# Weight sums by accumulating DMA, another order of Strassen's products, and another order of the last units of a feed-forward network

## Chip, core and metric

The kernel runs on one core of a Trainium2 chip. The metric is the device time of one execution in microseconds (us), the median of several runs. The core has five instruction queues that matter here. TensorE (PE in the profile, with PEld for its weight loads) does the matmuls. VectorE (DVE) and ScalarE (ACT) do elementwise work. GpSimd (POOL) does small work and can issue DMA transfers. SyncE (SP) issues most of the loads. Each queue is worked off in order. A DMA issued from any queue runs on the same 16 DMA engines.

## The reference

Two decoder layers over 256 tokens of width 1024, in float32. Cut to the part that the change touches:

```python
def swiglu(x, w1, w3, w2):
    return (jax.nn.silu(x @ w1) * (x @ w3)) @ w2

for i in range(DEPTH):                     # DEPTH = 2
    h = h + 0.5 * swiglu(rms_norm(h, g_ffn1[i]), w1_a[i], w3_a[i], w2_a[i])
    u = rms_norm(h, g_mix[i])
    h = h + hybrid_mixer(u, ...)           # three attention branches, gates, w_out
    h = h + 0.5 * swiglu(rms_norm(h, g_ffn2[i]), w1_b[i], w3_b[i], w2_b[i])
    h = h + sigmoid(rms_norm(h, g_ple[i]) @ w_ple_gate[i]) * (p[i] @ w_ple_proj[i])
out = rms_norm(h, g_final)
```

The hidden width of the feed-forward network (FFN) is 2816. There are four FFNs in a run: layer 0 a and b, layer 1 a and b.

## The kernel before

**Precision.** Every float32 operand is split into a high and a low float32r part: an ACT cast makes the high part (`whi`, `xhi`, `fhi`), and a DVE subtraction the low one (`wlo`, `xlo`, `flo`). One product is then three matmuls (`mm3`, lines 102 to 104). Weights come in tiles of 128 x 1024 (512 KB). `load` (lines 85 to 87) loads one into `raw` (4 buffers) and splits it; `split_w` splits a tile that is in SBUF already, through `split_T` (lines 135 and 136). Both write into the same 7 pairs of `whi` and `wlo`, so ACT and DVE can run at most 7 tiles ahead of TensorE.

**One FFN.** `ffn` cuts the hidden width into 11 chunks of 256 columns. For a chunk c, "up" makes the 256 gate columns and the 256 value columns side by side (512 columns) from all of D = 1024, for both blocks of 128 tokens. `gated` makes silu(gate) times value of one token block: an ACT activation, then a DVE operation into `pr` (lines 236 to 238). `turn(c)` transposes the two `pr` tiles of a chunk on TensorE (line 250, four transposes) and splits the result into `fhi` and `flo`. `down_unit(c, j)` loads one tile of w2 and adds its product with half a chunk to the four `acc` banks of PSUM (12 matmuls). Chunks 0 to 2 go up in the ordinary way at the start of the FFN; chunks 3 to 6 go up in quarters, `up_unit(c, i, os)` (one weight tile, 12 matmuls each).

**Strassen pairs.** Chunks 7 and 8, and 9 and 10, are made in pairs. The input is seen as a 2 x 2 matrix of blocks (token block by half of D), and the weights of two chunks as a 2 x 2 matrix of quarters (half of D by chunk, two 128 x 1024 tiles each). Seven products of quarters stand for eight. `x_forms` makes the sums of the input once per FFN. `winograd` loads the eight weight tiles of a pair (`wr`, line 317), `form` makes sums of quarters with DVE (line 320, in place or into `t2s`), `make(i)` splits the operand of product i, and the generator `products` runs the products: 12 matmuls each, into a PSUM bank of the tag `tr`, which the transposes use as well (2 banks). Line 345 adds a bank to an earlier result on DVE, and line 352 copies product 1 out on ACT.

**Order.** `block` writes the order out by hand. In step k it calls `make` for the product after next in its list, `form(k + 2)`, the next product, one quarter of an ordinary up, and a unit of down and turns as its two dictionaries say. One call to `block` covers one pair; an FFN has two calls. The second pair's loads are issued in step 6 of the first block. After the second block come the down units of chunks 5 and 6 with turns 6, 10 and 9 among them, and last the downs of chunks 9 and 10, which close the four `acc` banks one after the other. The framework puts waits where the data need them, hands out buffers as they come free, and may move independent instructions within a queue; the order above is its starting point.

**Beyond the FFN.** `mixer` does the attention branches and `ple` the embedding gate. `norm_r` (lines 164 to 175) computes the factor of the next RMSNorm from the finished rows, with small operations on POOL.

Of the kernel before, what the change touches and what calls it, by code (L numbers as in the profile page):

```python
# [33 lines left out]
def trunk(ctx: ExitStack, tc: tile.TileContext, a: dict, out: bass.AP):  # L34
# [10 lines left out]
    def nm(s):  # L45
        n_tile[0] += 1
        return f"{s}_{n_tile[0]}"
# [143 lines left out]
    def ffn(li, w13, w2, r, g, first=False, aside=None):  # L191
        nonlocal ident
        with tc.tile_pool(name=nm("fp"), bufs=3) as fp:

            def wtile():
                return fp.tile([P, U], F32, tag="wr", name=nm("wr"), bufs=10)

            def t512(name):
                return fp.tile([P, 512], F32, tag="t512", name=nm(name), bufs=4)
# [67 lines left out]
            def x_forms():  # L267
# [31 lines left out]
                V.tensor_tensor(out=s1, in0=a10, in1=a11, op=ALU.add)  # L299
# [5 lines left out]
                sub(a01, a01, s1)  # L305
# [5 lines left out]
            def winograd(c, fx):  # L311
                ws, t2s, fw = [], [], {}
                for u in range(2):
                    ws.append({(kh, nh): wtile() for kh in range(2) for nh in range(2)})
                for kh, nh in ((0, 0), (1, 0), (0, 1), (1, 1)):
                    for u in range(2):
                        nc.sync.dma_start(ws[u][kh, nh], w13[li, c + nh, 2 * kh + u])

                def sub(out, a, b):
                    V.tensor_tensor(out=out, in0=a, in1=b, op=ALU.subtract)  # L320


                def form(i):
                    for u, w in enumerate(ws):
                        if i == 1:
                            sub(w[0, 0], w[0, 1], w[0, 0])
                        elif i == 2:
                            t2s.append(wtile())
                            sub(t2s[u], w[1, 1], w[0, 0])
                        elif i == 3:  # L330
                            sub(w[0, 1], w[1, 1], w[0, 1])
                        else:
                            sub(w[1, 0], w[1, 0], t2s[u])
# [10 lines left out]
                def add(out, a, b):  # L344
                    V.tensor_tensor(out=out, in0=a, in1=b, op=ALU.add)


                def products():
                    o = bank_tr()
# [7 lines left out]
                    o = bank_tr()  # L357
# [7 lines left out]
                    o = bank_tr()  # L365
                    product(o, 5, True)
                    c22 = t512("c22")
                    add(c22, o, m1)
                    gated(c + 1, 1, c22, r[0])
                    yield  # L370
                    product(o, 3)
                    add(u2, o, u2)
                    gated(c + 1, 0, u2, r[0])
                    yield
                    o = bank_tr()
                    product(o, 4, True)
                    add(m1, o, m1)
# [3 lines left out]
                return make, form, products()  # L381


            def block(wg, plain, turns, downs, then=None):
                make, form, ps = wg
                following = None
                os = []
                for k in range(8):
                    if k < 6:
                        make((2, 6, 7, 5, 3, 4)[k])  # L390
                    if k < 3:
                        form(k + 2)
                    if k == 6 and then is not None:
                        following = winograd(then, fx)
                    if k == 7 and then is not None:
                        following[0](1)
                        following[1](1)
                    if k < 7:
                        next(ps)
                    if k % 4 == 0:  # L400
                        os = []
                    up_unit(plain[k // 4], k % 4, os)
                    if k in downs:
                        down_unit(*downs[k])
                    for t in turns.get(k, ()):
                        turn(t)
                return following

            for c in range(3):
# [21 lines left out]
            wg[1](1)  # L431
            for j in range(2):
                down_unit(0, j)
            if first:
                later()
            wg = block(
                wg, (3, 4), {0: [2], 4: [3]},
                {0: (1, 0), 1: (1, 1), 2: (2, 0), 3: (2, 1), 5: (3, 0), 6: (3, 1)}, 9,
            )
            if aside is not None:  # L440
                aside()
            block(
                wg, (5, 6), {0: [4], 1: [7], 2: [8], 5: [5]},
                {1: (4, 0), 2: (4, 1), 3: (7, 0), 4: (7, 1), 5: (8, 0), 6: (8, 1)},
            )
# [673 lines left out]
```

## Time and profile before

| | before |
|---|---|
| median of 3 runs | 1333.01 us (1332.68 to 1333.23) |
| the profiled execution, its time | 1332.86 us |
| its span, first to last instruction | 1331.1 us |
| TensorE matmul busy | 1312.2 us, 6624 matmuls |
| TensorE weight loads busy | 1097.5 us |
| VectorE busy | 994.0 us |
| ScalarE busy | 802.8 us |
| GpSimd busy | 50.2 us |
| read from HBM | 234.40 MB |
| granted TensorE clock | 0.998 |

Busy time is the time in which an engine executed an instruction; matmuls overlap each other, so a busy TensorE may still be issuing more slowly than it could. A row of a group reads: line, engine, operation, out<-in with the program's names, count, then busy time in us, mean ns of one, idle time of the engine just before them and what ended it. A row of the timeline reads: start in us, duration in us, engine, line, operation, count, and in brackets the idle time before it with the instruction that ended it.

### The profile page before, as it was taken

To read this page: it belongs to the slowest core of one execution; us is meant where nothing else is said; L and a number is where in the kernel's file an instruction comes from. 1 tells how busy PE (TensorE), PEld (TensorE's weight loads), DVE (VectorE), ACT (ScalarE), POOL (GpSimd) and SP (SyncE) were. 2 spreads that over 40 slices of the span, in tenths; PEclk is the share of its full clock that TensorE was granted. 3 is DMA by queue.
4 is the path that set the end of the run, shared out by engine and by line. 5 is a ranking of instruction groups with operands and counts; after the bars stand their busy time and mean duration, and the time that the engine had idled before them with its cause. 6 is when DMAs were issued, how large, how long until landed. Compare 5 with 4: busy or idle time off the path is not lost.

```text
span 1331.1 us, 17969 instructions
## 1 busy us (share of the span) xinstructions
PE 1312.2 (99%) x6624; PEld 1097.5 (82%) x6624; DVE 994.0 (75%) x1414; ACT 802.8 (60%) x1205; POOL 50.2 (4%) x109
## 2 busy tenths in 40 slices
PE   9999999999999999999999999999999999999997
PEld 7788879978888888887888888898888788888876
DVE  7998755666768789975789986566676677999755
ACT  6665546665775655654756665466667835655645
POOL 1000000001100000000100000000010000000001
PEclk9999999999999999999999999999999999999999
DMA  8774537534455567455566646373444465583542
GB/s 296 274 269 127 187 103 228 171 123 132 147 169 175 161 227 276 122 164 182 163 239 196 217 128 210 103 224 127 159 142 143 144 204 167 206 299 102 180 145 80
DMA packets 67769, 236.63 MB, mean 178 GB/s; under 512 B 8160, under 2 KB 8800, under 8 KB 67680
## 3 DMA queue, kind: packets, MB, share of 16 engines
q1 hardware_dynamic: 67104, 234.39, 54.0%
q8 instruction: 52, 0.85, 0.3%
q10 hardware_dynamic: 576, 1.08, 0.2%
q14 instruction: 37, 0.30, 0.1%
HBM read 234.40 MB, written 1.05 MB: 177 GB/s over the span
## 4 chain that ended last, share of the span: by engine, by line
PE 94%; ACT 2%; DVE 2%; DMA 1%; issue 1%; POOL 0%; SPq 0%; POOLq 0%; ACTq 0%; DVEq 0%
PE mm L102 17%; PE mm L104 17%; PE mm L103 17%; PE acc L102 8%; PE acc L103 8%; PE acc L104 8%; PE tr L104 4%; PE tr L102 4%; PE tr L103 4%; PE tr L250 1%; PE tr L150 1%; ACT whi L86 1%; PE tr L716 1%; DVE wlo L87 1%; DMA h<-in_x 1%
## 5 line engine op out<-in xcount | busy, mean ns | idle before, releaser
L87 DVE TENSOR_TENSOR wlo<-raw,whi 128x1024 fp32r<-128x1024 f32 (+1 forms) x378 | 450.1, 1201 | 137.3 <-ACT whi L86 135.1
L86 ACT CAST whi<-raw 128x1024 fp32r<-128x1024 f32 (+1 forms) x378 | 387.3, 1035 | 198.2 <-PE mm L104 77.5
L102 PE MATMUL mm<-whi,xhi 128*128 128x512 f32 (+1 forms) x760 | 296.0, 393 | 0.0
L103 PE MATMUL mm<-wlo,xhi 128*128 128x512 f32 (+1 forms) x760 | 295.1, 389 | 0.3 <-DVE wlo L87 0.3
L104 PE MATMUL mm<-whi,xlo 128*128 128x512 f32 (+1 forms) x760 | 295.2, 389 | 0.0
L102 PEld LDWEIGHTS mm<-whi,xhi 128*128 128x128 f32 x760 | 143.0, 188 | 30.0 <-DVE sqk L516 0.7
L104 PEld LDWEIGHTS mm<-whi,xlo 128*128 128x128 f32 x760 | 142.8, 188 | 29.7 <-DVE xlo L136 0.7
L103 PEld LDWEIGHTS mm<-wlo,xhi 128*128 128x128 f32 x760 | 142.9, 188 | 28.9 <-DVE wlo L87 0.8
L135 ACT CAST whi<-wr 128x1024 fp32r<-128x1024 f32 (+1 forms) x120 | 121.6, 1023 | 66.9 <-PE acc L104 38.9
L136 DVE TENSOR_TENSOR wlo<-wr,whi 128x1024 fp32r<-128x1024 f32 (+1 forms) x120 | 140.6, 1185 | 24.8 <-ACT whi L135 23.6
L102 PE MATMUL acc<-whi,fhi 128*128 128x512 f32 x352 | 132.0, 393 | 7.7 <-ACT fhi L135 7.7
L103 PE MATMUL acc<-wlo,fhi 128*128 128x512 f32 x352 | 137.9, 392 | 0.4 <-DVE wlo L87 0.4
L104 PE MATMUL acc<-whi,flo 128*128 128x512 f32 x352 | 134.6, 390 | 0.0
L102 PEld LDWEIGHTS acc<-whi,fhi 128*128 128x128 f32 x352 | 65.7, 188 | 23.2 <-ACT fhi L135 9.6
L103 PEld LDWEIGHTS acc<-wlo,fhi 128*128 128x128 f32 x352 | 66.1, 188 | 15.2 <-DVE wlo L87 1.8
L104 PEld LDWEIGHTS acc<-whi,flo 128*128 128x128 f32 x352 | 66.1, 188 | 13.6
L320 DVE TENSOR_TENSOR wr<-wr,wr 128x1024 f32<-128x1024 f32 x64 | 76.3, 1217 | 0.0
L102 PE MATMUL mm<-xhi,whi 128*128 128x256 f32 x256 | 73.8, 288 | 0.0
L104 PE MATMUL mm<-xhi,wlo 128*128 128x256 f32 x256 | 72.5, 283 | 0.0
L103 PE MATMUL mm<-xlo,whi 128*128 128x256 f32 x256 | 72.4, 283 | 0.0
L102 PE MATMUL tr<-whi,q 128*128 128x512 f32 x160 | 63.7, 398 | 0.0
L104 PE MATMUL tr<-whi,q 128*128 128x512 f32 x160 | 62.6, 391 | 0.0
(248 smaller groups left out, 1960.8 us busy)
## 6 DMA issues: line engine op xcount, KB each, us to landing
raw<-in_w13b SPq DMA_DIRECT2D x56, 512.0 KB, 3.7
raw<-in_w13a SPq DMA_DIRECT2D x52, 512.0 KB, 4.2
raw<-in_wg SPq DMA_DIRECT2D x48, 512.0 KB, 3.7
raw<-in_w2a SPq DMA_DIRECT2D x44, 512.0 KB, 4.4
raw<-in_w2b SPq DMA_DIRECT2D x44, 512.0 KB, 4.3
wr<-in_w13a SPq DMA_DIRECT2D x32, 512.0 KB, 6.7
raw<-in_wqk SPq DMA_DIRECT2D x32, 512.0 KB, 4.1
wr<-in_w13b SPq DMA_DIRECT2D x32, 512.0 KB, 6.2
```

What stands on the lines that cost most here:

```text
L86: A.copy(hi[:, c], raw[:, c])
L87: V.tensor_tensor(out=lo[:, c], in0=raw[:, c], in1=hi[:, c].bitcast(F32), op=ALU.subtract)
L102: PE.matmul(o, lhs[0], rhs[0], start=first, stop=False, **more)
L103: PE.matmul(o, lhs[0], rhs[1], start=False, stop=False, **more)
L104: PE.matmul(o, lhs[1], rhs[0], start=False, stop=last, **more)
L135: A.copy(hi, t)
L136: V.tensor_tensor(out=lo, in0=t, in1=hi.bitcast(F32), op=ALU.subtract)
L150: PE.transpose(t[:, j * P : (j + 1) * P], h[tb][:, k * P : (k + 1) * P], ident)
L250: PE.transpose(t[:, j * S + tb * P : j * S + (tb + 1) * P], prs[c, tb][:, j * P : (j + 1) * P], ident)
L320: V.tensor_tensor(out=out, in0=a, in1=b, op=ALU.subtract)
L716: PE.transpose(t[:, j * P : (j + 1) * P], e[:, j * P : (j + 1) * P], ident)
```

## The change

`winograd` becomes `pair`. It loads a pair's quarters into x (upper half of D, first chunk), y (lower, first), w (upper, second) and z (lower, second), and makes sums of quarters in place by DMA transfers on POOL's queue that add a tile from memory to the tile in SBUF: w + upper first (for product 5), then w + lower second (6), then w + lower first (4); z + upper second (7). `form`, `t2s` and the DVE subtractions of line 320 go. A sum is issued after the split of the tile's earlier content. Signs in `x_forms` change with it, and so does the order of the products: 1, 2, 5, 3, 6, 7, 4 instead of 1, 2, 6, 7, 5, 3, 4. Products 5 and 3 are copied out by ACT and later subtracted on DVE. The first pair's tiles are loaded in the order w, x, y, z. The second pair's loads are issued one quarter at a time, with the products 5, 3, 6 and 7 (steps 2 to 5). `wr` gets 12 buffers instead of 10, `t512` 5 instead of 4.

`block` now walks a list: S is the next Strassen product, P a quarter of an ordinary up, D a unit of down, T a turn. The units behind the blocks stand in another order as well.

```diff
             def wtile():
-                return fp.tile([P, U], F32, tag="wr", name=nm("wr"), bufs=10)
+                return fp.tile([P, U], F32, tag="wr", name=nm("wr"), bufs=12)
...
-                V.tensor_tensor(out=s1, in0=a10, in1=a11, op=ALU.add)
+                sub(s1, a10, a11)
...
-                sub(a01, a01, s1)
+                V.tensor_tensor(out=a01, in0=a01, in1=s1, op=ALU.add)
...
+            ORDER = (1, 2, 5, 3, 6, 7, 4)
+
+            def pair(c, bank):
+                def at(kh, nh, u):
+                    return w13[li, c + nh, 2 * kh + u]
+
+                t = {q: [wtile() for _ in range(2)] for q in "xywz"}
+                fw = {}
+                quarters = {"x": (0, 0), "y": (1, 0), "w": (0, 1), "z": (1, 1)}
+
+                def fetch(q):
                     for u in range(2):
-                        nc.sync.dma_start(ws[u][kh, nh], w13[li, c + nh, 2 * kh + u])
...
+                        nc.sync.dma_start(t[q][u], at(*quarters[q], u))
+
+                def plus(q, kh, nh):
+                    for u in range(2):
+                        nc.gpsimd.dma_start(t[q][u], at(kh, nh, u), accum_op=ALU.add)
 
                 def make(i):
-                    at = {1: (0, 0), 2: (1, 0), 7: (0, 1), 5: (0, 0), 3: (1, 1), 4: (1, 0)}
-                    fw[i] = [split_w(t2s[u] if i == 6 else w[at[i]]) for u, w in enumerate(ws)]
+                    q = {1: "x", 2: "y", 5: "w", 3: "z", 6: "w", 7: "z", 4: "w"}[i]
+                    fw[i] = [split_w(w) for w in t[q]]
+                    if i == 5:
+                        plus("w", 1, 1)
+                    elif i == 3:
+                        plus("z", 0, 1)
+                    elif i == 6:
+                        plus("w", 1, 0)
...
+                    product(o, 5, True)
+                    c5 = t512("c5")
+                    A.copy(c5, o)
+                    yield
+                    product(o, 3)
+                    v = t512("v")
+                    A.copy(v, o)
+                    yield
+                    o = bank()
                     product(o, 6, True)
                     u2 = t512("u2")
-                    add(u2, o, m1)
+                    sum_(u2, o, m1)
+                    sum_(v, v, u2, ALU.subtract)
+                    gated(c + 1, 0, v, r[0])
                     yield
                     product(o, 7)
-                    add(m1, o, m1)
+                    sum_(m1, o, m1)
+                    sum_(c5, c5, m1, ALU.subtract)
+                    gated(c + 1, 1, c5, r[0])
...
+                for kind, *arg in plan:
+                    if kind == "S":
+                        if k < 6:
+                            make(ORDER[k + 1])
+                        if then is not None:
+                            if k == 2:
+                                following = pair(*then)
+                                following[1]("w")
+                            elif k == 3:
+                                following[1]("x")
+                                following[2]()
...
-                    wg = winograd(7, fx)
+                    wg = pair(7, bank_tr)
+                    for q in "wxyz":
+                        wg[1](q)
+                    wg[2]()
...
+            wg = block(wg, [
+                ("S",), ("P", 3, 0), ("D", 1, 0), ("T", 2), ("S",), ("P", 3, 1), ("D", 1, 1), ("S",),
+                ("P", 3, 2), ("D", 2, 0), ("S",), ("P", 3, 3), ("D", 2, 1), ("S",), ("P", 4, 0), ("T", 3),
+                ("S",), ("P", 4, 1), ("D", 3, 0), ("S",), ("P", 4, 2), ("D", 3, 1), ("P", 4, 3),
+            ], (9, bank_tr))
...
+            wg = block(wg, [
+                ("S",), ("P", 5, 0), ("T", 4), ("S",), ("P", 5, 1), ("D", 4, 0), ("T", 7), ("S",), ("P", 5, 2),
+                ("D", 4, 1), ("T", 8), ("S",), ("P", 5, 3), ("D", 7, 0), ("S",), ("P", 6, 0), ("D", 7, 1),
+                ("S",), ("P", 6, 1), ("T", 5), ("D", 8, 0), ("S",), ("P", 6, 2), ("D", 8, 1), ("P", 6, 3),
+            ])
...
-            for j in range(2):
-                down_unit(5, j)
-            turn(6)
-            turn(10)
-            for j in range(2):
-                down_unit(6, j)
-            turn(9)
+            block((None, None, None, iter(())), [
+                ("D", 5, 0), ("T", 10), ("D", 5, 1), ("T", 6), ("T", 9), ("D", 6, 0), ("D", 6, 1),
+            ])
```

`first_sum`, the third function that `pair` returns, is `plus("w", 0, 0)`.

More of the change, by code (lines that the diff above doesn't have):

```diff
@@ L195, in wtile @@
             def wtile():
-                return fp.tile([P, U], F32, tag="wr", name=nm("wr"), bufs=10)
+                return fp.tile([P, U], F32, tag="wr", name=nm("wr"), bufs=12)
             def t512(name):
-                return fp.tile([P, 512], F32, tag="t512", name=nm(name), bufs=4)
+                return fp.tile([P, 512], F32, tag="t512", name=nm(name), bufs=5)
             if first:
@@ L342, in product, with sum_ @@
                         mm3(o, [y[:, kt, :] for y in fx[i]], m, start and kt == 0, kt == 3, skip_group_check=True)
-                def add(out, a, b):
-                    V.tensor_tensor(out=out, in0=a, in1=b, op=ALU.add)
+                def sum_(out, a, b, op=ALU.add):
+                    V.tensor_tensor(out=out, in0=a, in1=b, op=op)
                 def products():
-                    o = bank_tr()
+                    o = bank()
                     product(o, 1, True)
@@ L356, in products @@
                     yield
-                    o = bank_tr()
+                    o = bank()
+                    product(o, 5, True)
[6 more added lines that the diff above has]
+                    yield
+                    o = bank()
                     product(o, 6, True)
                     u2 = t512("u2")
-                    add(u2, o, m1)
+                    sum_(u2, o, m1)
@@ L361, in products @@
+                    sum_(v, v, u2, ALU.subtract)
+                    gated(c + 1, 0, v, r[0])
                     yield
                     product(o, 7)
-                    add(m1, o, m1)
+                    sum_(m1, o, m1)
+                    sum_(c5, c5, m1, ALU.subtract)
+                    gated(c + 1, 1, c5, r[0])
                     yield
[L365 to L375, printed above, removed]
+                    o = bank()
                     product(o, 4, True)
-                    add(m1, o, m1)
+                    sum_(m1, o, m1)
                     gated(c, 1, m1, r[0])
                     yield
-                return make, form, products()
@@ L384, in block, with first_sum @@
-            def block(wg, plain, turns, downs, then=None):
-                make, form, ps = wg
+                def first_sum():
+                    plus("w", 0, 0)
+                return make, fetch, first_sum, products()
+            def block(now, plan, then=None):
+                make, _, _, ps = now
                 following = None
                 os = []
[L388 to L398, printed above, removed]
-                        next(ps)
[L400 to L406, printed above, removed]
+                k = 0
+                for kind, *arg in plan:
[9 more added lines that the diff above has]
+                                following[2]()
+                            elif k == 4:
+                                following[1]("y")
+                            elif k == 5:
+                                following[1]("z")
+                            elif k == 6:
+                                following[0](1)
+                        next(ps)
+                        k += 1
+                    elif kind == "P":
+                        if arg[1] == 0:
+                            os = []
+                        up_unit(*arg, os)
+                    elif kind == "D":
+                        down_unit(*arg)
+                    else:
+                        turn(*arg)
@@ L430, in ffn @@
             wg[0](1)
-            wg[1](1)
             for j in range(2):
```

26 lines of the change are left out of this document (removed).

## The prediction

> **What bounds the kernel now.** I read the page first: busy times and the group of each matmul line. Then busy time by window over one feed-forward stage, the waits, and the timeline of the places where TensorE stood still.
>
> ```profile
> PE 1312.2 (99%) x6624; PEld 1097.5 (82%) x6624; DVE 994.0 (75%) x1414; ACT 802.8 (60%) x1205; POOL 50.2 (4%) x109
> ...
> L102 PE MATMUL acc<-whi,fhi 128*128 128x512 f32 x352 | 132.0, 393 | 7.7 <-ACT fhi L135 7.7
> ...
> L320 DVE TENSOR_TENSOR wr<-wr,wr 128x1024 f32<-128x1024 f32 x64 | 76.3, 1217 | 0.0
> ```
> ```profile
> 701.00:764.00 63.00, 63.00 (x283) 51.91 (x282) 60.10 (x61) 38.43 (x45) 0.00 (x0) 1.00 0.61 201
> 764.00:831.00 67.00, 66.34 (x305) 54.76 (x303) 50.39 (x55) 39.56 (x48) 0.00 (x0) 1.00 0.55 167
> ```
>
> The window rows give start:end, length, then busy time of PE, PEld, DVE, ACT and POOL with their counts, granted clock, DMA share and GB/s. They cover the two Strassen blocks of the third FFN. TensorE is the bound. In the first block it never rests: 63 us hold 283 matmuls, one every 63 / 283 = 0.223 us, so a unit of 12 matmuls takes 2.67 us. The clock is granted in full. DVE is close behind (60.10 of 63), but nobody waits for it there. The change keeps every matmul: seven products a pair, the same up and down units, the same transposes. So it can only win time in which TensorE stands, and 1331.1 - 1312.2 = 18.9 us of visible idle is a ceiling, most of it outside the edited code. Inside it, two kinds of stall matter.
>
> The first is at the end of each FFN:
>
> ```profile
> PE acc L102 <- ACT fhi L135: 7.7, 8, 1.2
> ```
> ```profile
> 121.17 0.60 PE L250 MATMUL tr<-ident,pr 128*128 128x128 f32 x4
> 121.52 0.48 PE L102 MATMUL tr<-whi,q 128*128 128x512 f32 x1
> ```
> ```profile
> 171.59 1.04 PE L250 MATMUL tr<-ident,pr 128*128 128x128 f32 x8
> 171.78 1.05 ACT L86 CAST whi<-raw 128x1024 fp32r<-128x1024 f32 x1 [1.67 <-PE acc L104]
> 172.74 1.07 ACT L135 CAST fhi<-tr 128x512 fp32r<-128x512 f32 x2
> 173.37 0.50 PE L102 MATMUL acc<-whi,fhi 128*128 128x512 f32 x1 [0.74 <-ACT fhi L135]
> ...
> 178.96 0.60 PE L250 MATMUL tr<-ident,pr 128*128 128x128 f32 x4
> 179.16 1.04 ACT L86 CAST whi<-raw 128x1024 fp32r<-128x1024 f32 x1 [1.67 <-PE acc L104]
> 180.11 0.58 ACT L135 CAST fhi<-tr 128x512 fp32r<-128x512 f32 x1
> 180.74 0.50 PE L102 MATMUL acc<-whi,fhi 128*128 128x512 f32 x1 [1.18 <-ACT fhi L135]
> ```
>
> The waits row reads: in total, times, longest. Eight stalls, two in each of four FFNs. A turn (four transposes) is followed at once by a down matmul that reads what the turn made, and the cast of it sits behind a 1.05 us weight cast that the last down released. Where other work follows a turn, the next matmul starts 0.35 us after the first transpose (121.17 to 121.52); at the last turn it starts 1.78 us after (178.96 to 180.74). The last turn loses 1.78 - 0.35 = 1.43 us start to start, 1.18 of it as visible idle.
>
> The second is the start of the first block of layer 0, three short stalls:
>
> ```profile
> 46.17 0.50 PE L102 MATMUL tr<-whi,xhi 128*128 128x512 f32 x1 [0.56 <-ACT m L352]
> 47.09 0.50 PE L103 MATMUL acc<-wlo,fhi 128*128 128x512 f32 x1 [0.41 <-DVE wlo L87]
> ...
> 55.63 0.50 PE L103 MATMUL mm<-wlo,xhi 128*128 128x512 f32 x1 [0.33 <-DVE wlo L87]
> ```
>
> **The change, part by part.**
>
> *The tail.* Before: both units of down 5, turn 6, turn 10, both of down 6, turn 9, then the last downs, which begin with chunk 9. After: a unit of 5, turn 10, a unit of 5, turn 6, turn 9, both units of 6, the last downs. Turn 9 now has two units, 5.3 us, ahead of its first reader; the 1.2 us from weight cast to end of its cast fits. Turn 6 is still followed by one other turn and then by its own down, as turn 6 and turn 10 were: the 0.74 us stall stays. Gain 4 x 1.43 = 5.7 us (4 x 1.18 = 4.7 by visible idle, the lower end). The loads and casts of the tail are the same ones; turn 10, now alone, costs what turn 9 alone cost.
>
> *Sums off DVE.* 64 tensor operations of 1217 ns go (the L320 row), 76.3 us of DVE. They lie beside TensorE, so they gain nothing by themselves, except the two stalls on DVE wlo above: 0.41 + 0.33 = 0.74 us, once.
>
> *Sums by DMA.* Each pair gets eight transfers of 512 KB on POOL's queue that add into a tile that a plain load, or an earlier sum, filled. Before, POOL issued no DMA, so their price has to be bounded.
>
> ```profile
> 10.00:20.00 10.00, 10.00 (x46) 8.29 (x45) 8.48 (x14) 6.83 (x15) 3.87 (x3) 1.00 1.03 411
> ```
> ```profile
> raw<-in_w13b SPq DMA_DIRECT2D x56, 512.0 KB, 3.7
> ...
> wr<-in_w13a SPq DMA_DIRECT2D x32, 512.0 KB, 6.7
> wr<-in_w13b SPq DMA_DIRECT2D x32, 512.0 KB, 6.2
> ```
> ```profile
> DMA to landing us min/median/max: 4.0/6.4/9.9
> ```
>
> With the DMA engines full, 411 GB/s: a 512 KB load holds them 0.524 MB / 411 GB/s = 1.28 us. Low end 1.28 us of engine time and 4.0 us to landing; high end 9.9 us, the longest landing of a load into these tiles. I take the wr row, 6.4 us to landing, as the nearest (same tile, same size, in a queue). A sum that is needed has this long:
>
> ```profile
> 121.36 1.05 ACT L135 CAST whi<-wr 128x1024 fp32r<-128x1024 f32 x1 [1.67 <-PE acc L104]
> ...
> 130.01 1.05 ACT L135 CAST whi<-wr 128x1024 fp32r<-128x1024 f32 x1 [1.67 <-PE acc L104]
> ...
> 138.65 1.05 ACT L135 CAST whi<-wr 128x1024 fp32r<-128x1024 f32 x1 [1.31 <-PE acc L104]
> ```
> ```profile
> 124.28 1.23 DVE L136 TENSOR_TENSOR wlo<-wr,whi 128x1024 fp32r<-128x1024 f32 x1
> ```
>
> Casts of successive products start 8.65 us apart (121.36, 130.01, 138.65). In the new order a tile is split, added into and split again two products later: w for 5, 6 and 4, z for 3 and 7. The last reader of the first split ends at 124.28 + 1.23 = 125.51, the second following cast starts at 138.65: 13.1 us for two transfers. At 6.4 us, even one after the other (12.8), they fit: price nothing. That cover gone, ACT stands in its queue ahead of the next turn's cast; the shortest way from a turn to its down (turn 3, turn 4) is two units, 5.3 us. So TensorE stops only when two transfers take over 13.1 + 5.3 = 18.4 us. At the high end, 2 x 9.9 = 19.8, it loses 1.4 us in each of 24 chains (three a pair): 34 us.
>
> Engine time: block one has the DMA busy 0.61 of 63 us, 24.6 us free; it issues eight sums, so each may hold the engines 3.1 us. The rule that speaks against the change is in the Trainium skill, "Collectives: The Full Stack", Part 3, on the fold count: an add in the DMA reads two sources through the same read ring, so it runs at half a copy's rate. By it a sum would hold the engines 2.56 us, eight of them 20.5 of the 24.6 free us, and the sum here would not move except at the starts below; by the row alone it is 10.2 us. No run before shows which.
>
> *Loads in another order, 12 tiles for 10.* The first pair's loads now go w, x, y, z, where x, the first product's quarter, went first; and the two sums into w compete with x, y, z.
>
> ```profile
> 474.30 8.60 SPq L317 DMA_DIRECT2D wr<-in_w13b  x8
> ```
> ```profile
> 483.65 1.99 ACT L135 CAST whi<-wr 128x1024 fp32r<-128x1024 f32 x2
> 485.54 2.00 ACT L86 CAST whi<-raw 128x1024 fp32r<-128x1024 f32 x2
> ```
> ```profile
> 29.64 8.99 SPq L317 DMA_DIRECT2D wr<-in_w13a  x8
> ```
> ```profile
> 39.01 2.00 ACT L135 CAST whi<-wr 128x1024 fp32r<-128x1024 f32 x2
> ```
> ```profile
> 30.00:40.00 10.00, 10.00 (x46) 8.24 (x45) 9.21 (x17) 5.48 (x10) 0.00 (x0) 1.00 1.02 382
> 40.00:50.00 10.00, 9.04 (x42) 6.75 (x41) 9.89 (x11) 8.66 (x13) 0.00 (x0) 1.00 0.99 370
> ```
>
> Second FFN: issue at 474.30, landing about 6.2 later, cast at 483.65: 3.1 us in hand. Two loads ahead take 2 x 1.28 = 2.56; a sum sharing the engines up to 1.28 more: x up to 0.7 us late. Behind it in ACT's queue stand the casts of down 0 (485.54), needed about 2 us later. Price between 0 and 0.7; I take 0.2 in each of three FFNs, since part of the lateness is met by that slack. Layer 0: 39.01 - 29.64 - 6.7 = 2.7 us in hand, but the DMA is full (1.02, 0.99): the two sums push later loads back by 2 x 1.28 = 2.6 us. Price between -0.74 (only the DVE stalls gone) and 2.6 + 0.1; I take +0.6. Total of the starts +1.2. The second pair's loads are now spread over four products instead of issued after the sixth: nothing, they were in time before.
>
> *Smaller things.* Products 5 and 3 each leave by a 0.59 us ACT copy, 16 copies in all; ACT has 24.6 of 63 us free, so nothing. DVE has five 128x512 operations a pair as before.
>
> ```profile
> L345 DVE TENSOR_TENSOR m<-tr,m 128x512 f32<-128x512 f32 x16 | 10.9, 684 | 0.0
> ...
> L580 DVE TENSOR_TENSOR merged<-merged,xg 128x512 f32<-128x512 f32 x16 | 11.0, 688 | 0.2
> ```
>
> Two of them now read SBUF only: 688 against 684 ns. The chains of chunks 8 and 10 grow by one such operation; their turns come four or more units later, so nothing. Signs in the x forms change, not their count. POOL queues its sums behind the splits that they overwrite; behind them on POOL stand only later sums and the norms at an FFN's end:
>
> ```profile
> POOL ss L171 <- ACT junk L164: 904.1, 17, 174.6
> ```
>
> POOL waits 904 us for those norms already; the last sum is issued tens of microseconds ahead of them.
>
> *Sum.* The profiled execution took 1332.86 us (span 1331.1), 0.15 below the median of 1333.01. 1332.86 - 5.7 + 1.2 = 1328.4 us.
>
> **The rivals.**
> *Better than forecast, chance 0.12.* x is in time everywhere (-1.2, and -0.74), and turn 6 loses less, since ACT may reach its cast earlier: 0.74 x 4 = 3.0 at most. 1332.86 - 5.7 - 0.7 - 3.0 = 1323.5. Against it: the order around turn 6 has the same form as before.
> *The starts eat the gain, 0.18.* If sums hold the engines twice as long as loads (the page's rule above is this case), x is late by another 1.28 us: 2.0 us in three FFNs, and layer 0 loses 5.1. 1332.86 - 5.7 + 6.0 + 5.1 = 1338 if TensorE feels all of it; with half, 1332.7, no change. For it: layer 0's DMA share of 1.0; against: 2 us of slack behind x, and other units that can run first.
> *Slower, 0.20: sums land too late in the blocks.* Decided by one number, two sums in over 18.4 us. At 20 us for two it costs 1.6 x 24 = 38 us: 1328.4 + 38 = 1366. For it: nothing of POOL's DMA is shown, and ACT's queue is strict. Against: plain loads of this size land in 6.4 us.
> *The sums gain nothing and cost nothing* is inside the forecast: the DVE time was hidden.
>
> **How the numbers follow.** Forecast 0.50 (1326.5 to 1330.5 is its own range: 4.7 to 5.7 from the tail, -0.7 to +2.3 at the starts). With the better case, faster by over 0.2% (2.67 us, about what a measurement can tell) is 0.62; the starts give most of "same", 0.18; the late sums 0.20. The range runs from 1323.5, the better case's end, to 1339, just past the starts' full price; of the late sums nearly all lies outside.
>
> **What would show it.** Right: the waits of TensorE for ACT fhi at L102 fall from 8 to 4 and from 7.7 to about 3.0 us; the next matmul after the last turn follows without idle; the L320 group is gone and DVE is some 76 us less busy while the windows of the blocks still show PE at full; a POOL DMA queue with 64 transfers, about 34 MB, landing under 6.5 us. The starts are wrong if PE idles for ACT or DVE at the first products, or if the raw loads there land late. Wrong altogether: ACT waiting for DMA at the splits of products 6, 7 and 4, and PE holes in mid-block.

## The result, and the profile after

The changed kernel is slower: 1366.24 us (median of 3 runs, 1362.22 to 1369.69) against 1333.01 us (1332.68 to 1333.23). The ratio is 1.0248, with a 95% interval of 1.0203 to 1.0293. The profiled execution of it took 1369.69 us with a span of 1367.9, 36.8 us more than the 1331.1 of before. All medians and ratios in this document are of undisturbed executions; one execution of e10 (5980.37 us) and one of the kernel before beside it (1868.25 us) were far slower than the others and are left out.

The page of the changed kernel, busy times, DMA queues and the costliest groups:

```profile
PE 1326.2 (97%) x6624; PEld 1106.2 (81%) x6624; DVE 928.8 (68%) x1350; ACT 806.3 (59%) x1221; POOL 104.7 (8%) x173
...
q1 hardware_dynamic: 67104, 234.39, 51.3%
q0 software_dynamic: 9216, 33.56, 13.0%
...
PE 76%; DMA 13%; issue 5%; DVE 2%; ACT 2%; POOL 1%; SPq 0%; POOLq 0%; ACTq 0%; DVEq 0%
...
L102 PE MATMUL mm<-whi,xhi 128*128 128x512 f32 (+1 forms) x760 | 300.5, 397 | 12.4 <-DVE pr L238 11.6
...
L102 PE MATMUL acc<-whi,fhi 128*128 128x512 f32 x352 | 136.9, 394 | 3.0 <-ACT fhi L135 3.0
...
L102 PE MATMUL tr<-whi,q 128*128 128x512 f32 x160 | 67.3, 421 | 14.2 <-DVE u L346 14.1
...
wr<-in_w13a SPq DMA_DIRECT2D x32, 512.0 KB, 9.5
wr<-in_w13a POOLq DMA_DIRECT2D x32, 512.0 KB, 11.0
```

The same 6624 matmuls run. The row with the shares is that of the chain that ended last: the profile follows the last instruction back, at each step to what released it. TensorE holds 76% of this chain and DMA 13%. Before:

```profile
PE 94%; ACT 2%; DVE 2%; DMA 1%; issue 1%; POOL 0%; SPq 0%; POOLq 0%; ACTq 0%; DVEq 0%
```

The wait of the downs for `fhi` fell from 7.7 to 3.0 us, as forecast for the tail; two new groups of TensorE waits, for a DVE operation that empties a PSUM bank (11.6 and 14.1 us), are larger than that. The queue rows give packets, MB and share of 16 engines: SP's 234.39 MB take 51.3% of the DMA engines' time, POOL's 33.56 MB take 13.0%. Per MB a sum costs (13.0 / 33.56) / (51.3 / 234.39) = 1.77 times a load. From issue to landing a sum takes 11.0 us at the median, the plain loads into the same tiles 9.5 instead of 6.7.

The windows of both Strassen blocks of the second FFN and of the first block of the third follow (columns as before; a DMA share of 1.0 or a little more means full). The changed kernel comes to these blocks later, 14.8 us at the second FFN and 21.9 at the third. So each window runs here between the same two matmuls, by count, that bound the windows of 63 and 67 us before:

```profile
501.90:573.70 71.80, 66.92 (x284) 54.22 (x283) 47.23 (x50) 40.12 (x48) 7.02 (x8) 0.95 0.87 263
573.70:640.30 66.60, 66.60 (x307) 55.12 (x306) 47.59 (x51) 39.72 (x49) 5.21 (x6) 1.00 0.77 212
```
```profile
723.20:795.20 72.00, 65.59 (x281) 53.37 (x280) 47.70 (x49) 40.37 (x48) 7.02 (x8) 0.95 0.86 260
```

The first block takes about 72 us instead of 63. Its DMA engines are busy for 0.87 x 71.8 = 62.5 us, where 0.61 x 63 = 38.4 was enough before. POOL issues eight sums in it: six of the first pair, and the first sum of the second pair, which is two transfers. DVE is relieved (60.10 to 47.70 us in the first block of the third FFN), and it buys nothing. Where the DMA is full it moves 311 GB/s (from 500 to 550 us, row further below), and a full DMA of plain loads moved 411. In the second block six sums are issued, the DMA share is 0.77, and TensorE never rests (66.60 of 66.60): sums in themselves do not stop it.

Comparing the start of the n-th matmul in the two traces tells where the time went: TensorE falls back by 15.2 us in the blocks of the first FFN, by 8.8, 9.3 and 8.5 us in those of the other three, 41.8 in all; each FFN's tail wins 1.5 to 1.6 us back, and the start of layer 0 costs 1.0. Two stalls an FFN make up most of it. The first FFN's two on TensorE, and behind them what ACT and DVE did in the same stretch (timeline):

```profile
91.75 0.79 PE L102 MATMUL mm<-whi,xhi 128*128 128x512 f32 x1 [5.38 <-DVE pr L238]
101.72 0.80 PE L102 MATMUL tr<-whi,q 128*128 128x512 f32 x1 [4.22 <-DVE u L346]
```
```profile
86.17 1.04 ACT L135 CAST whi<-wr 128x1024 fp32r<-128x1024 f32 x1 [3.88 <-DMA wr<-in_w13a]
...
89.00 1.04 ACT L86 CAST whi<-raw 128x1024 fp32r<-128x1024 f32 x1 [1.29 <-DMA raw<-in_w13a]
89.95 0.83 ACT L236 ACTIVATE act<-mm,r 128x256 f32<-128x256 f32 x2
...
97.62 1.04 ACT L135 CAST whi<-wr 128x1024 fp32r<-128x1024 f32 x1 [2.70 <-DMA wr<-in_w13a]
```
```profile
91.22 0.87 DVE L238 SCALAR_TENSOR_TENSOR pr<-mm,r,act 128x256 f32<-128x256 f32 x2
...
100.98 0.68 DVE L346 TENSOR_TENSOR u<-tr,m 128x512 f32<-128x512 f32 x1
```

Read it from the back. TensorE at 91.75 needs a PSUM bank that the first of the two `pr` operations begun at 91.22 frees. `pr` needs the activation of 89.95, and that stands in ACT's queue behind the casts at 86.17 and 89.00, which each waited for a DMA: the first for a sum, the second for an ordinary load. So TensorE does not wait for the product whose operand is late; it waits for an eviction of other work, queued on ACT behind the late cast. The waits of the whole run say the same:

```profile
ACT whi L135 <- DMA wr<-in_w13a: 29.7, 10, 4.4
ACT whi L135 <- DMA wr<-in_w13b: 29.5, 9, 4.7
...
PE tr L102 <- DVE u L346: 14.1, 4, 4.9
...
PE mm L102 <- DVE pr L238: 11.6, 4, 5.4
...
ACT whi L86 <- DMA raw<-in_w13a: 3.0, 4, 1.3
```

In the trace, each of the 19 waits of the first two rows ends when a sum of POOL's queue lands; none is for a plain load. They are 59.2 us in all. In the kernel before, ACT never waited for a `w13` tile in `wr`. Ordinary loads into `raw` are late too, but they kept ACT waiting for few us (last row; `w2a` 0.7, `w13b` not at all).

A stall also slows what follows. Clock of the 4.8 us behind the first stall, and of an undisturbed stretch ahead of it:

```profile
91.70:96.50 4.80, 4.75 (x11) 3.79 (x12) 1.61 (x2) 1.04 (x1) 0.00 (x0) 0.50 1.03 325
80.00:86.00 6.00, 6.00 (x29) 4.93 (x27) 1.23 (x1) 1.05 (x1) 0.00 (x0) 1.00 1.06 274
```

Eleven matmuls took 4.8 us at a granted clock of 0.50; at the pace of the second row (6.00 / 29) they would take 2.3. The eight stalls cost 27.0 us from start to start, above the usual distance of two matmuls. The clock records of the trace show seven stretches at 0.50, each beginning within or just behind one of them; the shortest stall, 1.52 us at 766.08, has none. The halved clock and smaller stops are the other 14.8 of the 41.8.

### The profile page after: what moved, and what is told of

Same layout as the page of the kernel before. It is cut to its first block, busy times and chain, and to the rows that moved or that the text cites. A ratio compares the mean times of both kernels' runs of the same rounds, so it can differ in the third digit from the quotient of the medians.

```text
span 1367.9 us, 18109 instructions
## 1 busy us (share of the span) xinstructions
PE 1326.2 (97%) x6624; PEld 1106.2 (81%) x6624; DVE 928.8 (68%) x1350; ACT 806.3 (59%) x1221; POOL 104.7 (8%) x173
## 3 DMA queue, kind: packets, MB, share of 16 engines
q1 hardware_dynamic: 67104, 234.39, 51.3%
q0 software_dynamic: 9216, 33.56, 13.0%
## 4 chain that ended last, share of the span: by engine, by line
PE 76%; DMA 13%; issue 5%; DVE 2%; ACT 2%; POOL 1%; SPq 0%; POOLq 0%; ACTq 0%; DVEq 0%
PE mm L102 14%; PE mm L104 14%; PE mm L103 14%; PE acc L102 7%; PE acc L104 7%; PE acc L103 7%; DMA wr<-in_w13b 6%; PE tr L102 3%; PE tr L103 3%; PE tr L104 3%; DMA wr<-in_w13a 2%; DMA raw<-in_w13a 2%; DMA raw<-in_w2a 2%; DVE wlo L87 2%; ACT whi L86 1%
## 5 line engine op out<-in xcount | busy, mean ns | idle before, releaser
L102 PE MATMUL mm<-whi,xhi 128*128 128x512 f32 (+1 forms) x760 | 300.5, 397 | 12.4 <-DVE pr L238 11.6
L102 PE MATMUL acc<-whi,fhi 128*128 128x512 f32 x352 | 136.9, 394 | 3.0 <-ACT fhi L135 3.0
L102 PE MATMUL tr<-whi,q 128*128 128x512 f32 x160 | 67.3, 421 | 14.2 <-DVE u L346 14.1
L102 PEld LDWEIGHTS acc<-whi,fhi 128*128 128x128 f32 x352 | 65.8, 188 | 17.7 <-ACT fhi L135 3.9
L103 PE MATMUL tr<-wlo,q 128*128 128x512 f32 x160 | 65.4, 409 | 0.0
L104 PE MATMUL tr<-whi,q 128*128 128x512 f32 x160 | 65.0, 407 | 0.0
```

The source lines that it names most:

```text
L102: PE.matmul(o, lhs[0], rhs[0], start=first, stop=False, **more)
L103: PE.matmul(o, lhs[0], rhs[1], start=False, stop=False, **more)
L104: PE.matmul(o, lhs[1], rhs[0], start=False, stop=last, **more)
```

## The experiments

Three causes could make the blocks late: the engine time of the sums, which fills the DMA; the number, queue and order of the transfers, whatever they do; or the new order of products and evictions, which has nothing to do with DMA. The runs take them apart. Ratios are to the kernel before on the same chip, with their 95% intervals.

| run | us (range) | ratio |
|---|---|---|
| e1, e2: before, other tails | 1327.69 (1326.63–1328.68); 1323.26 (1322.27–1323.88) | 0.9957 (0.9945–0.9970); 0.9925 (0.9912–0.9937) |
| e3: after, copies for sums | 1326.75 (1326.60–1327.94) | 0.9951 (0.9936–0.9966) |
| e4: after, sums on DVE | 1329.40 (1327.74–1331.74) | 0.9973 (0.9963–0.9982) |
| e5, e8: after, loads held; with e2's tail | 1373.81 (1371.12–1377.62); 1369.87 (1366.47–1372.60) | 1.0303 (1.0287–1.0320); 1.0268 (1.0254–1.0282) |
| e7: after, 10 tiles | 1367.97 (1364.16–1370.67) | 1.0255 (1.0239–1.0272) |
| e9, e11: after, first sum on DVE; with e2's tail | 1343.09 (1342.56–1345.17); 1338.37 (1336.97–1340.86) | 1.0072 (1.0057–1.0087); 1.0042 (1.0030–1.0055) |
| e10: before, idle copies | 1344.54 (1342.12–1347.83) | 1.0086 (1.0069–1.0103) |
| e12: e5 and e9 together | 1364.08 (1361.45–1367.50) | 1.0238 (1.0216–1.0259) |

### The tail alone (e1, e2)

```diff
 (before)
-            for j in range(2):
-                down_unit(5, j)
-            turn(6)
+            down_unit(5, 0)
             turn(10)
+            down_unit(5, 1)
+            turn(6)
+            turn(9)
             for j in range(2):
                 down_unit(6, j)
-            turn(9)
```

> The kernel before with only the new order of the last units: a unit of down 5, turn 10, a unit of 5, turn 6, turn 9, both units of 6. No sum by DMA, products in the old order. If the step of the prediction on the tail holds, 4 x 1.43 = 5.7 us are won: 1327.3 us, and the waits of TensorE for ACT fhi fall from 8 (7.7 us) to 4 (about 3.0 us). Rival: what the last turn saves comes back at the first downs of chunks 9 and 10 or in the mixer's first loads: 1333.

In e2 turn 6 and turn 10 follow the first unit of 5, and turn 9 alone the second.

> The kernel before with both turns that are followed by their own down moved: a unit of 5, turn 6, turn 10, a unit of 5, turn 9, both units of 6. If the 0.74 us stall before down 6 has the same cause as the one at turn 9 (the cast behind a weight cast), both go: another 4 x 1.0 us start to start, 1333.0 - 5.7 - 4.0 = 1323.3 us, and no wait for ACT fhi is left at those places. Rival: turn 6 right after one unit now waits for the gate of chunk 6 itself, which is made only after the last up: no better than the tail-only kernel, 1327.

e1 measured 1332.98 - 1327.69 = 5.3 us, e2 9.7. The group of the downs in e1 and then in e2:

```profile
L102 PE MATMUL acc<-whi,fhi 128*128 128x512 f32 x352 | 132.1, 394 | 3.0 <-ACT fhi L135 3.0
```
```profile
L102 PE MATMUL acc<-whi,fhi 128*128 128x512 f32 x352 | 131.9, 393 | 0.0
```

From 7.7 to 3.0 to 0.0 us: the step on the tail is right, and with a unit behind each turn turn 6's wait goes too. e2 beats both kernels, and nothing else that ran beats e2.

### What of the sums is dear (e3, e4)

```diff
 (after, e3: the transfers load their tile over the old content; the sums are left out)
-                        nc.gpsimd.dma_start(t[q][u], at(kh, nh, u), accum_op=ALU.add)
+                        nc.gpsimd.dma_start(t[q][u], at(kh, nh, u))
```

> The changed kernel, its 64 transfers on POOL's queue left as they are but copying over the tile where they added into it; so the sums are left out. Theory A (a sum holds the DMA engines about twice as long as a copy, and the first block fills them): ten transfers a block each get some 1.3 us shorter, 13 of 62 us of engine time in the first block come free, the stalls of 5 to 10 us per FFN shrink to under a third: 1325 to 1337 us. Theory B (a transfer issued by POOL is slow in itself, whatever it does): the stalls stay, 1355 to 1370.

```diff
 (after, e4: the same four sums from tiles that are in SBUF, by DVE)
-                def plus(q, kh, nh):
+                def plus(q, a, op=ALU.add, b=None):
                     for u in range(2):
-                        nc.gpsimd.dma_start(t[q][u], at(kh, nh, u), accum_op=ALU.add)
+                        V.tensor_tensor(out=t[q][u], in0=t[b or q][u], in1=t[a][u], op=op)
```

> The changed kernel with the same order of products, units and loads and the same buffers, but its sums made by DVE out of the loaded quarters (w+x, then +z, then +y; z becomes w-x): eight DVE operations a pair as in the kernel before, no transfer on POOL's queue. Theory A and B (the DMA sums are the cause): the stalls in the first blocks go, only the tail's gain stays, 1327 us, at most 2 us off. Theory C (the new order of products with its copies by ACT and longer chains makes the stalls): 1350 or more.

e3, its POOL queue, its transfers and the first block of the second FFN:

```profile
q0 software_dynamic: 9216, 33.56, 7.0%
...
wr<-in_w13a POOLq DMA_DIRECT2D x32, 512.0 KB, 7.2
```
```profile
486.20:549.10 62.90, 62.90 (x284) 51.99 (x283) 47.40 (x50) 40.58 (x47) 4.20 (x8) 1.00 0.76 289
```

The same 9216 packets and 33.56 MB in the same queue, behind the same splits, take 7.0% of the engines' time instead of 13.0, the share in the same block falls from 0.87 of 71.8 us to 0.76 of 62.9, the stalls of the blocks are gone, and 1326.75 us is e1's tail and a microsecond more. The number, queue and order of the transfers are not the cause; that they add is. e4 has the new products and evictions without any DMA sum: the stalls in the blocks are gone here too. One stop of 2.33 us is left at layer 0's start, about its distance to e1 (1.7 us); e9 and e12, whose first sum is on DVE as well, have the same stop, and e3 does not. The order of products and evictions is not the cause.

### The price of a sum by itself (e6)

This kernel leaves out the whole computation and only moves 512 KB tiles: a load and a sum alone, eight loads, eight sums, both side by side, loads on two queues.

> Only transfers of 512 KB and a few DVE operations that set them apart, none of the reference's computation: one load, one sum by DMA, eight loads from SP, eight sums from POOL, eight loads beside eight sums, eight loads on each of both queues. Theory A: loads land 1.25 us apart; sums about 2.5 apart, twice a load; a load and a sum side by side 3.8 us per pair; loads on both queues 1.25 us apart. Theory B: loads issued by POOL are as slow as sums. One sum alone: 4 to 6 us to landing.

Lone transfers, then windows with loads only, with sums only, and with loads on both queues (here the columns are length, DVE, POOL, clock, DMA share, GB/s):

```profile
one<-in_w13a SPq DMA_DIRECT2D x1, 512.0 KB, 3.3
one<-in_w13a POOLq DMA_DIRECT2D x1, 512.0 KB, 5.3
```
```profile
20.40:23.80 3.40, 2.33 (x2) 0.00 (x0) 1.00 1.01 412
38.00:52.00 14.00, 7.15 (x7) 1.19 (x2) 1.00 1.07 211
108.80:122.00 13.20, 7.40 (x7) 0.00 (x0) 1.00 1.03 414
```

With the engines full, loads move 412 GB/s on one queue and 414 on two, sums 211 of counted bytes. Loads land 1.26 us apart once the queue is full, sums 2.53: a sum holds the engines for twice a load's time. The Trainium skill gives the same factor for adds in the DMA ("Collectives: The Full Stack", Part 3, on the fold count: two sources through one read ring). It is stated there for collectives; here 2.53 / 1.26 = 2.0 agrees with it for a sum into SBUF, and no run here shows the ring. Side by side, a load and a sum took 3.8 us a pair, the two prices added.

Now the first block's bill can be drawn up from bytes. In the second FFN, 263 GB/s over 71.8 us are 18.9 MB, 36 tiles of 0.524 MB. Ten sums land in the block: the eight that are issued in it, and the two transfers of the first pair's first sum, issued 6 to 8 us ahead of it. That is 10 x 2.53 + 26 x 1.26 = 58.1 us, and TensorE needs only 63 for the block. The transfers do not come evenly:

```profile
500.00:550.00 50.00, 47.63 (x208) 38.50 (x207) 31.07 (x30) 26.41 (x33) 7.02 (x8) 0.97 1.05 311
```

From 500 to 550, 311 GB/s are 29.7 tiles, and with the ten sums among them 25.3 + 19.7 x 1.26 = 50.1 us of 50: full on end. The ten are issued between 494.2 and 534.1 us and land between 503.7 and 549.9, all in this stretch.

### Fewer sums, other places (e5, e7, e8, e9, e11, e12)

```diff
 (after, e5: each quarter's load of the second pair waits for the split made just before it)
+                        if behind is not None:
...
+                            tc.add_manual_dep(ins.ins, behind.ins.name, order, reason="held")
...
-                                following[1]("w")
+                                following[1]("w", split[0])
 (e7: bufs=12 to 10 for wr;  e8: e5 with e2's tail)
 (e9: the first of the four sums on DVE, 48 DMA sums are left;  e11: e9 with e2's tail)
-                    plus("w", 0, 0)
+                    for u in range(2):
+                        V.tensor_tensor(out=t["w"][u], in0=t["w"][u], in1=t["x"][u], op=ALU.add)
 (e12: e5 and e9, the second pair's DVE sum issued in step 6)
```

> The changed kernel, all 64 sums by DMA kept, but each quarter of the second pair's loads held until the split of the first pair that stands beside it in the program is done (w behind the split for product 3, x behind 6, y behind 7, z behind 4). Theory A1 (bunching: with 12 buffers the second pair's eight loads and its first sums were issued some 15 to 40 us before their need, ahead of the sums and raw loads that TensorE needed first): block one needs 22 loads x 1.28 + 8 sums x 2.56 = 48.6 of 57 us, so held apart it fits: 1326 to 1335 us. Theory A2 (the block's transfers are too many in any order): the stalls stay near 5 us or more per FFN, 1345 to 1366.

> The changed kernel with 10 buffers for the weight quarters, as before, in place of 12. Theory A1: the second pair gets its last tiles only when the first pair's are free, so fewer loads run ahead of the needed sums: between the changed kernel and the held one, 1335 to 1358. Theory A2: no better, 1360 to 1370, since the count of transfers is the same; below 1330 would say that the two added buffers alone made the loss.

> The held kernel with the tail order of the second experiment (turn 6 after the first unit of down 5, turn 9 after the second). If the held loads cost nothing, this meets or beats the kernel before with that tail (1323.3): 1322 to 1324, since DVE has 76 us less to do at the start of layer 0. Under A2, 1340 or more.

> The changed kernel with the first sum of a pair (w + upper first) made by DVE from the two loaded tiles; the other three of the four sums stay with the DMA, 48 transfers in place of 64. Budget theory (loads at 1.26 us and sums at 2.53 us each, as measured alone, filled the 63 us ahead of and in the first block: 30 x 1.26 + 10 x 2.53 = 63.1): six sums are left there, 30 x 1.26 + 6 x 2.53 = 53.0 of 63, and the stalls go: 1326 to 1332 us. Rival (the chain of sums into one tile, each waiting for the split before and landing late, is what costs, at any load): the chain w, 6, 4 is still there, half the loss or more stays, 1345 to 1360.

> As the run with the first sum on DVE, with the tail order of the second experiment. If the budget theory holds, this is the tail-both kernel with 57 us of DVE work less: 1322 to 1326 us, level with 1323.3 within a few us since TensorE does not wait for DVE outside layer 0's start. Under the rival, 1340 to 1356.

> The changed kernel with two edits at once: the first of the four sums of a pair (w plus the upper quarter) is made on VectorE, in step 6, and the second pair's loads are each held behind the weight split made just before them. With the first edit alone (e9) the six sums and twenty loads before 542 us still filled the DMA for 40.4 of 43 us, and it was nearly idle afterwards. Budget theory: now the same transfers (30 loads at 1.26 us and 6 sums at 2.53 us, 53 us) are spread over the 63 us, nothing is late, and the time is that of the tail alone: 1326 to 1332 us, no wait of TensorE over 1 us in mid-block. Rival, a sum is late even on a DMA with room, because two of them in a chain and the issue on POOL's queue behind the splits take longer than the chain leaves: 1340 us or more, with the waits at the products that read a sum.

e5 and e7 move the same transfers about and win nothing; e5 is slower than both of its forecasts. Its DMA is as busy in the first block of the second FFN (0.86 of 74.2 us, where the changed kernel has 0.87 of 71.8), and it has one stall of about 9 us an FFN in place of two smaller ones:

```profile
500.40:574.60 74.20, 65.67 (x284) 53.84 (x283) 47.39 (x50) 40.59 (x48) 7.01 (x8) 0.93 0.86 253
```
```profile
PE tr L102 <- DVE u L351: 36.8, 4, 10.4
```

With all sums on the DMA, issuing the second pair's loads later in this way does not help. e8, with e2's tail, is as far behind (1369.87). e9 has six DMA sums in the block and lands between its two forecasts, at 1343, and e11 at 1338 as well. I had expected e9 to be well, at 53 of 63 us by a count of its transfers. By the n-th matmul it falls back 3.3 us at layer 0's start, where its first sum is on DVE, and 13.4 us in the four first blocks, where the changed kernel lost 41.8. Two windows of e9, then the full stretch of e3 in the same block:

```profile
500.00:542.00 42.00, 39.82 (x177) 32.49 (x176) 30.25 (x30) 24.29 (x28) 5.25 (x6) 1.00 0.98 297
542.00:550.00 8.00, 8.00 (x36) 6.61 (x37) 7.96 (x11) 4.44 (x7) 0.00 (x0) 1.00 0.42 132
```
```profile
496.00:526.00 30.00, 30.00 (x136) 24.80 (x136) 20.49 (x20) 17.17 (x21) 4.20 (x8) 1.00 1.02 412
```

The mean over a block hides it. In e9 the DMA is full for some 40 us on end and less than half busy after; in e3 it is full for 30 us and then catches up, and TensorE never stops; in the changed kernel, in the window shown above, it is full for 50. The ordinary loads into `raw` are late in each of these stretches. Between 500 and 542 they took 6.1 us to landing in e3, 12.3 in e9 and 13.4 in the changed kernel (medians). In e3's full stretch alone it was 10.8, and ACT waited only 0.5 us for loads of `w13` into `raw` in its whole run. In e9 ACT waited 17.7 us for sums and 23.4 us for the ordinary loads of `w13` over the whole run. So with six sums, too, the transfers come late enough to stop ACT. How long a full stretch the block bears is bounded by these runs only: 30 us of copies cost nothing, 40 us with six sums among them did.

e12 was to spread the six sums over the block. It measured 1364 and does not answer that question, for two reasons of its own making. A held load stops SP's queue, with the ordinary loads behind it (SP issued nothing from 76.5 to 92.6 us), so the transfers still came in a lump, in the first FFN from 58 to 91 us; and the second pair's sum on DVE came ahead of other work in DVE's queue and waited there for its late tile:

```profile
58.00:91.00 33.00, 28.24 (x125) 23.06 (x123) 16.79 (x16) 18.28 (x22) 5.38 (x6) 1.00 0.98 278
```
```profile
87.66 1.23 DVE L392 TENSOR_TENSOR wr<-wr,wr 128x1024 f32<-128x1024 f32 x1 [11.15 <-DMA wr<-in_w13a]
```
```profile
94.12 0.80 PE L102 MATMUL mm<-whi,xhi 128*128 128x512 f32 x1 [7.88 <-DVE pr L240]
```

Whether six well spread sums would fit in the first block stays open. The second blocks of the changed kernel say that they can fit where there is room: there six sums land 5.5 to 8.0 us after issue (second FFN), and TensorE never rests. The hold in e5 and e8 has the first of these faults too.

### Late loads or late sums (e10, e13)

```diff
 (before: four idle copies a step in five steps of each first block, behind a split, into 2 tiles nobody reads)
+                    if k < 5 and then is not None:
+                        for j in range(4):
+                            spare = fp.tile([P, U], F32, tag="spare", name=nm("spare"), bufs=2)
+                            ins = nc.gpsimd.dma_start(spare, w13[li, j, k % 4])
...
+                            tc.add_manual_dep(ins.ins, split[0].ins.name, order, reason="load")
```

Twenty copies at 1.26 us hold the DMA as long as ten sums, and nobody waits for them: what is lost is lost by the lateness of the other loads.

> The kernel before, sums on DVE and old order and tail, plus 20 copies of 512 KB on POOL's queue in each first block into tiles that nobody reads, two in flight, four behind each of the first five steps' splits: 20 x 1.26 = 25 us of engine time per first block, what the ten sums hold. If the late raw loads in a full DMA are what stops TensorE, it loses as the changed kernel does: 1350 to 1375. If what stops it is ACT standing in its queue for the sums themselves, and raw loads have enough in hand, this costs little: 1333 to 1340.

> The kernel before with 20 idle copies of 512 KB per first block on POOL's queue, as in e10, for its profile alone. Contention theory: the DMA share of the first blocks goes from 0.61 to about 1.0, the loads into raw land 10 us or more later than before, and TensorE waits in the middle of the block for casts that wait for these loads. If instead the raw loads stay under 6 us and the lost time lies elsewhere, e10's loss was not lateness of the loads. Time 1340 to 1350 us.

e10 measured 1344.54 us, 11.5 more than the 1333.06 before on its chip, at a point between its two forecasts. The trace is that of e13, the same kernel again (one execution, 1349.34 us, span 1347.6). In the second FFN: the window, TensorE's stop, and ACT's just before it; then what ACT waited for in the whole run.

```profile
515.00:542.00 27.00, 25.12 (x113) 20.47 (x111) 17.14 (x19) 11.55 (x14) 3.74 (x8) 1.00 1.03 418
```
```profile
542.55 0.50 PE L102 MATMUL acc<-whi,fhi 128*128 128x512 f32 x1 [2.44 <-ACT fhi L135]
```
```profile
540.97 1.04 ACT L86 CAST whi<-raw 128x1024 fp32r<-128x1024 f32 x1 [6.90 <-DMA raw<-in_w13b]
541.92 0.58 ACT L135 CAST fhi<-tr 128x512 fp32r<-128x512 f32 x1
```
```profile
ACT whi L86 <- DMA raw<-in_w13b: 17.7, 4, 6.9
...
ACT whi L86 <- DMA raw<-in_w13a: 14.5, 5, 7.3
```

The load into `raw` issued at 526.3 landed at 540.9; between 515 and 545 these loads took 11.0 us to landing (median), 4.6 in the kernel before; that is 6.4 us later, less than the 10 that I had expected. ACT stood 6.90 us for one of them, with the turn's cast behind it, and TensorE 2.44. By the n-th matmul, e13 loses 1.3, 5.0, 5.0 and 3.4 us in the four FFNs' blocks, 14.7 us against the changed kernel's 41.8. So a full DMA can cost this block time without any late sum. The 14.7 us are not a share of the 41.8, though. ACT waited 32.2 us for loads of `w13` into `raw` in e13, and 3.0 us in the changed kernel, where it waited 59.2 us for sums. There the late sums stopped ACT, and behind them the late ordinary loads had time to land. What these would cost if the sums came in time is not shown. The match of the two kernels is rough as well: the spare copies have two tiles and are never more than two in flight, so they queue less deeply than the sums, and in the first FFN they cost almost nothing although its DMA share is 0.93.

## Why the prediction was wrong

The forecast was 1328.4 us and faster; it is 1366.24 and slower, outside the range.

**The tail** was right: 5.7 us forecast, 5.3 in e1, turn 6's stall left as said and `fhi` at 3.0 us. **DVE's relief** was right in being worth next to nothing. **The starts** were sized fairly: 0.6 forecast for layer 0, 1.0 measured; 0.2 lost for each other FFN, and there 0.1 to 0.2 was won.

**The step that failed is the price of the sums by DMA**, "price nothing", and within it the landing time of 6.4 us with the engine time that was to allow it: "24.6 us free; it issues eight sums, so each may hold the engines 3.1 us". Three things were wrong in it.

First the count. Eight sums are issued in the block, as the forecast said, but ten land in it: the two transfers of the first pair's first sum, issued at 494.2 and 496.1 us, land at 503.7 and 508.0, and the block begins at 501.9. The forecast priced these two at the starts alone. Its own free time allows ten sums 24.6 / 10 = 2.46 us each; a sum takes 2.53. By the rule of the Trainium skill that the forecast quotes (2.56 us), ten sums were, by that measure, over the limit before anything ran.

Second, the load after the change. Eight sums by that rule were 20.5 us on top of 38.4, 58.9 of 63, and the text went on with a landing time of 6.4 us, read from a DMA that was 0.61 busy. A landing time holds for the load at which it was measured. In the changed kernel the sums took 11.0 us at the median (tiles of `w13a`; 10.5 for `w13b`), and the last six of the second FFN's block 15.8 to 21.5: three of these take longer each than the 18.4 us that the forecast had named for two as the point where TensorE stops. The point was usable, its input was not.

Third, the mean. By bytes the block's bill is 58.1 us of 63 and fits; but from 500 to 550 us the DMA was full on end, with all ten sums in this stretch. e9 shows as well that less than the whole block is too much when the transfers come in a lump: a block's share of 0.80 (494 to 559.9 us) was a stretch of 42 us at 0.98. (A share is not a bill, either: before, 201 GB/s over 63 us were 24 tiles, 30 us at 1.26, and the share said 38.4. That error made the forecast more careful, not less.)

The rival "sums land too late in the blocks" had the mechanism and, at 20 us for two, the time: 1366. The agreement of the number is luck. It counted 24 chains at 1.6 us each, in both blocks of an FFN. There are eight stalls of 1.7 to 5.5 us, all in the first blocks, seven of them with a halved clock beside the stall, which no rival named. The cover of "two units, 5.3 us" from a turn to its down was not what failed first, either: TensorE met a PSUM bank that ACT and DVE had not emptied. What the forecast named as the sign of being wrong, ACT waiting for DMA at the splits (19 times, 59.2 us) and TensorE holes in mid-block, is what the trace shows.

## What to carry to other kernels

A DMA that adds is no free vector engine: here it holds the 16 DMA engines twice as long as a copy of the same bytes. Before moving work to the DMA, draw up the engine time of every transfer in the stage, with those of the next stage that are issued early, and look at the fullest stretch rather than the mean of the stage; take landing times at the load after the change. When the DMA filled here, the first to stop was ACT, at a cast of a late tile, and TensorE then waited for a bank that has nothing to do with that tile, because its eviction stood behind the cast.

## What the runs showed of the hardware

- A sum of 512 KB from HBM into SBUF: 5.3 us to landing alone (a load 3.3), 2.53 us of all DMA engines when full (a load 1.26), and 864 ns on POOL to issue against 536 ns for a copy:

```profile
L75 POOL DMA_DIRECT2D d<-in_w13a x8 | 6.9, 864 | 24.6 <-DVE d L73 24.4
...
L90 POOL DMA_DIRECT2D f<-in_w13a x8 | 4.2, 536 | 33.9 <-DVE f L58 33.7
```

- The granted TensorE clock fell behind a stop of 2.37 us in the changed kernel: the stop, and the window behind it.

```profile
546.54 0.50 PE L102 MATMUL mm<-whi,xhi 128*128 128x512 f32 x1 [2.37 <-DVE pr L238]
```
```profile
546.50:551.00 4.50, 4.46 (x13) 3.46 (x14) 1.60 (x2) 1.67 (x3) 0.00 (x0) 0.62 1.02 358
```

The Trainium skill, "TensorE: Matmul & The Clock Gate", Part 1, puts the harmful gap above about 3.4 us; this one is under it and was followed by 0.62 over 4.5 us. A stop of 3.45 us in e7 was followed by 1.00, so the length of a stop alone did not decide it:

```profile
772.58 0.50 PE L102 MATMUL tr<-whi,q 128*128 128x512 f32 x1 [3.45 <-DVE u L346]
```
```profile
772.50:777.50 5.00, 4.92 (x22) 4.07 (x23) 5.00 (x8) 2.88 (x4) 0.00 (x0) 1.00 0.69 208
```
